# Expert weights loaded as runs of consecutive rows, with a permuted order of contraction

## The chip, the cores and the metric

The kernel runs on one core of one Trainium2 chip. The metric is the device time of one execution in microseconds, the median of several runs. A core has five engines that matter here: PE (TensorE, matmuls; its weight loads are shown apart as PEld), DVE (VectorE), ACT (ScalarE), POOL (GpSimd) and SP (SyncE, which here only issues DMAs). Loads run on 16 DMA engines that all queues share.

## The reference, cut to what matters

Two transformer blocks in float32 over 256 tokens of 1024 channels. The first block is attention, a layer norm, a mixture of experts and a second layer norm. The second block is a gated recurrence with a short convolution, then a feed-forward network. The change touches the mixture of experts:

```python
def moe_ffn(x, w_router, b_router, w_gu, b_gu, w_down, b_down):
    logits = xt @ w_router + b_router              # 256 tokens, 32 experts
    top_logit, top_e = lax.top_k(logits, 4)
    gate = jax.nn.softmax(top_logit, axis=-1)
    ...
    def expert_block(args):                        # xb: an expert's tokens
        h = xb @ w_gu[e] + b_gu[e]                 # w_gu[e]: 1024 x 2048
        h_gate, h_up = jnp.split(h, 2, axis=-1)
        h_gate = jnp.minimum(h_gate, 7.0)
        h_up = jnp.clip(h_up, -7.0, 7.0)
        act = h_gate * jax.nn.sigmoid(1.702 * h_gate) * (h_up + 1.0)
        return act @ w_down[e] + b_down[e]         # w_down[e]: 1024 x 1024
```

Each expert has 8 MiB of gate and up weights and 4 MiB of down weights, all float32, and every expert's weights are read once: 402.65 MB of the 477 MB that the kernel reads from HBM.

## The kernel before

Stages follow one another: attention (to about 115 us of the profile), layer norm and router, the 32 experts (about 140 to 1080 us), the second block (to the end). All large loads are issued by SP from one list, `loads`, in the order in which the weights are used. `pump` (L178) issues the next entries of the list; `weight` (L193) takes a loaded tile and pumps so many entries ahead. A tile is 128 partitions by 16 KiB (2 MiB). During the experts there are ten slots for them, six of pool `wa` (named `w` in the profile) and four of pool `wb`; a load waits until the matmuls on the slot's last content are done.

Expert weights are loaded by `load_rows` (L116). A tile of gate and up weights holds 256 rows of 2048 columns as two blocks: row `k*128 + p` of the piece goes to partition `p`, block `k`, so each partition receives two separate runs of 8 KiB. A tile of down weights holds 512 rows of 1024 columns as four blocks, four runs of 4 KiB to a partition. An expert takes four tiles of the first kind and two of the second. The second block's first weights, `w2`, come by `load_cols` (L105), 512 columns at a time, runs of 2 KiB. Contraction runs over partitions, so a matmul on block `k` needs the activations' channels `k*128 ... k*128+127` on the partitions.

An expert has 64 slots for tokens. Experts go in pairs (a batch). `make_batch` (L681) gathers the tokens of two experts with matmuls by a one-hot matrix: `gather` (L661) takes 128 channels of the normed tokens `h1` as the stationary operand and writes them, channel by partition, to `pgat`; `gathered` (L667) applies the norm's gain and bias on the way to `xs`. `gate_up` (L746) multiplies `xs` by the weights into banks `pg` and `pu` (L764); `swiglu` gives `at`, tokens by partition; `transpose_act` (L770) turns `at` in four pieces of 128 columns with PE (L773), `at` stationary and the identity moving; `down_half` (L780) multiplies by the down weights into `pd` (L786); `combine` (L804) adds the pair's results to the tokens (`pc`, L809). At expert 4 stands a run-time branch, `overflow` (L812), for experts with more than 64 tokens; it is not taken with these inputs, but every engine reads the condition (L815). `turn` (L490) turns `h1` for the router, `turn_router` multiplies the router's weights `wr` by the norm's gain, and `turn_parameters` (L348) turns the gains and biases so that channel `kt*128 + p` stands on partition `p`, column `kt` of `prm`.

A planner orders the instructions of each engine by its own costs and priorities, except in the stretches under `manual_schedule`, where the program's order holds. The experts' loop is left to the planner.

Of the kernel before, what the change touches and what calls it, by code (L numbers as in the profile page):

```python
# [10 lines left out]
F32 = mybir.dt.float32  # L11
# [11 lines left out]
P = 128  # L23
# [27 lines left out]
# columns of the constant table  # L51
# [3 lines left out]
def shape_constants():  # L55
    c = np.zeros((P, C_END), np.float32)
    r = np.arange(P)
    c[:, C_ID:C_ID + P] = np.eye(P)
    c[:, C_TRI:C_TRI + P] = r[:, None] < r[None, :]
    c[:, C_ONE:C_ONE + P] = 1.0  # L60
    c[:, C_IOTA:C_IOTA + P] = r[None, :]
    n = np.arange(256)
    half = BUCKETS // 2
    nf = np.maximum(n, 1).astype(np.float32)
    large = half + (np.log(nf / np.float32(half)) / np.float32(math.log(MAX_DIST / half))
                    * np.float32(BUCKETS - half)).astype(np.int32)
    bucket = np.where(n < half, n, np.minimum(large, BUCKETS - 1))
    onehot = (np.arange(BUCKETS)[:, None] == bucket[None, :]).astype(np.float32)
    # level lv: keys s of the even and queries t of the odd blocks of 2**lv; only those t stand
    masks = np.zeros((P, 7, P // 2), np.float32)  # L70
    s = r[:, None]
    for lv in range(7):
        H = 1 << lv
        t = r[r // H % 2 == 1][None, :]
        masks[:, lv] = (s // (2 * H) == t // (2 * H)) & (s // H % 2 == 0)
    return {"c_main": c, "c_bucket": onehot, "c_masks": masks.reshape(P, 7 * P // 2)}
# [7 lines left out]
def block_kernel(ctx: ExitStack, tc: tile.TileContext, a: dict, out: bass.AP, dbg=None):  # L84
# [14 lines left out]
    # ------------------------------------------------------------------ loads  # L99
# [22 lines left out]
    def load_rows_last(t, w, r0, n):  # L122
        """n = 4 blocks of rows, two of them alone"""
        cols = w.shape[1]
        v = t[:, 0:n * cols].rearrange("p (k c) -> p k c", c=cols)
        for k, m in ((0, 2), (2, 1), (3, 1)):
            nc.sync.dma_start(v[:, k:k + m], w[r0 + k * P:r0 + (k + m) * P, :]
                              .rearrange("(k p) c -> p k c", p=P))
# [14 lines left out]
    def open_room(t):  # L143
        """a slot without a load: room for what is computed"""
        nc.gpsimd.memset(t[:, 0:1], 0.0)
# [9 lines left out]
    for e in range(NE + 1):  # L155
        gu = [(("gu", e, c), load_rows, (w_gu[e], c * 256, 2)) for c in range(4) if e < NE]
        dn = [(("dn", e - 1, c), load_rows, (w_dn[e - 1], c * 512, 4)) for c in range(2) if e > 0]
        loads += dn + gu if e == OVF_AT else gu + dn
    end_moe = len(loads)
    loads[-1] = (loads[-1][0], load_rows_last, loads[-1][2])  # L160
# [43 lines left out]
    # R: 1 + slot of each token within its expert, 0 where it is not routed there  # L204
# [5 lines left out]
    # h1 is written late: its rows hold the tables of the relative bias until then  # L210
# [19 lines left out]
    # the second block's rows take its place  # L230
# [9 lines left out]
    nc.gpsimd.memset(eps_rms, RMS_EPS)  # L240
    R_LNG, R_LNB, R_PMIX, R_PFFN, R_NMIX, R_NFFN = (0, 1), (2, 3), 4, 5, 6, 7

    def bcast_row(psum_ap, r, half):
        """half of row r of `rows` on all partitions"""
        for q in range(2):
            c = 4 * r + 2 * half + q
            mm(psum_ap[:, q * 256:(q + 1) * 256], selb[:, c:c + 1].to_broadcast([96, P]), rows,
               start=True, stop=True)

    def passes(psum_ap, kts, *pairs):  # L250
        """the sum of all products of pairs of operands, pair by pair"""
# [10 lines left out]
    def warm(bank_, n):  # L262
        """n matmuls without a use, that open the clock gate"""
        for _ in range(n):
            mm(bank_[0:1, 0:T], idle, idle.to_broadcast([P, T]), start=True, stop=True)

    # ============================================================ attention
    with ExitStack() as c1:
# [9 lines left out]
        # constants and small parameters for later  # L278
# [8 lines left out]
        # per-channel parameters, 128 channels to a column  # L287
        fw = a["ffn_conv_w_2"][0].rearrange("j (k p) -> (j k) p", p=P)
        for r0, n, src in ((0, 8, a["ln_g"][0, 0:1]), (8, 8, a["ln_b"][0, 0:1])):
            nc.sync.dma_start(raw[r0:r0 + n, 0, :], src.rearrange("o (k p) -> (o k) p", p=P))  # L290
# [6 lines left out]
        # x turned to [channel, token]; matmuls before it and between open the clock gate  # L297
# [25 lines left out]
        nc.sync.dma_start(wr, a["moe_w_router"][0].rearrange("(k p) e -> p k e", p=P))  # L323
# [3 lines left out]
        def split3(dst, src):  # L327
            """dst rows 0.., 32.., 64..: three bf16 parts that sum to src exactly"""
# [19 lines left out]
        def turn_parameters(raw):  # L348
# [3 lines left out]
            V.tensor_copy(prm, pp)  # L352

        def turn_router():
            """the router behind the layer norm's gain and bias: its weights by the gain (wr),
            and its bias with the weights by the norm's bias (br)"""
# [21 lines left out]
        def proj_ch(pool, w, m, xh, xl, psum_ap):  # L378
            """psum [128 columns of w, T] = (columns m of w)^T x^T"""
# [3 lines left out]
        def proj_tok(pool, w, xh, xl, psums):  # L383
            """psums[tt] [128 tokens, 512] = x w for a chunk of 512 columns"""
# [9 lines left out]
        def attend(h, qT, kT):  # L394
# [19 lines left out]
            # columns: keys 0 of queries 0, keys 0 of queries 1, keys 1 of queries 1  # L414
# [48 lines left out]
        def stats(tt):  # L463
            """h1 = ALPHA x + attention and its statistics: mean, variance, 1 / deviation"""
# [14 lines left out]
        def scaled(tt, mv):  # L479
            """h1 = its layer norm but for gain and bias, half by half"""  # L480
# [9 lines left out]
        def turn(tt, hT, g):  # L490
            """half of the channels of a tile, turned to [channel, token]"""
            pt = ps.tile([P, 4, P], F32, name="htp", tag="v", bufs=2)
            for j in range(4):
                kt = 4 * g + j
                nc.tensor.transpose(pt[:, j, :], h1[:, tt, kt * P:(kt + 1) * P], ident)
            nc.scalar.copy(hT[:, 4 * g:4 * g + 4, :], pt)

        def logits(hT, n):
            """... after n matmuls that keep the clock gate open"""
# [8 lines left out]
        def choose(tt, lg):  # L508
            """the experts of a tile's tokens: sel, and one-hot in order"""
# [25 lines left out]
        # the rest for the first tile, then for the second  # L535
# [46 lines left out]
    # ============================================================ experts  # L582
    y = xtok
    with ExitStack() as c2:
# [10 lines left out]
        def gates():  # L595
            """the gates of each token's experts (G), and whether a load exceeds CAP"""
# [19 lines left out]
        def forget_bounds():  # L616
            """lower bound of the forget gates: running sum of the softmax over the layers
            less its first row; and 1 less the bound"""
# [8 lines left out]
        def start_y():  # L627
            """y = ALPHA * the layer norm + the experts' output biases by their gates"""
# [22 lines left out]
        # ---- experts, CAP slots each  # L651
# [9 lines left out]
        def gather(b, pg, kk, tt, j, start, stop):  # L661
            kt = 4 * kk + j
            mm(pg[:, j, :], h1[:, tt, kt * P:(kt + 1) * P],  # L663
# [3 lines left out]
        def gathered(xs, pg, kk):  # L667
            """the gathered channels with the layer norm's gain and bias"""
# [23 lines left out]
        def first_batch(choice):  # L692
            """batch 0, with the slots of the second tile's tokens found on the way"""
# [28 lines left out]
        def weigh_batch(b):  # L722
            """the gates of a batch, [slot, token]"""
# [46 lines left out]
        def transpose_act(at, tag="aT", copy=nc.any.tensor_copy):  # L770
            pt = bank("atp", [P, 4, P], "t")
            for j in range(4):
                nc.tensor.transpose(pt[:, j, :], at[:, j * P:(j + 1) * P], ident)  # L773
# [6 lines left out]
        def down_half(e, aT, pd, c):  # L780
            w = weight(("dn", e, c), AHEAD).rearrange("p (k c) -> p k c", c=D)
            for k in range(4):
                # rows c*512 + k*128 ..: block k of the activations' half c
# [28 lines left out]
        def overflow():  # L812
            """slots CAP.. of every expert, when one of them has more than CAP tokens"""
            n = nc.values_load(cnti[0:1, 0:1], min_val=0, max_val=NE)
            with tc.If(n > 0), tc.For_i(0, n, 1) as e:  # L815
                for g in range(2):
# [9 lines left out]
                    for kk in range(KT // 4):  # L826
                        pg = bank("opgat", [P, 4, P], "m")
                        for j in range(4):
                            kt = 4 * kk + j
                            for tt in range(NT):  # L830
                                mm(pg[:, j, :], h1[:, tt, kt * P:(kt + 1) * P], oh[:, tt],
# [16 lines left out]
                    for kt in range(KT):  # L848
                        for q in range(2):
                            w = p2.tile([P, FF], F32, name="ow", tag="ys")  # L850
                            nc.sync.dma_start(
                                w, w_gu[bass.ds(e, 1), kt * P:(kt + 1) * P, q * FF:(q + 1) * FF]
# [11 lines left out]
                    for kt in range(KT):  # L864
                        w = p2.tile([P, D], F32, name="owd", tag="ys")
                        nc.sync.dma_start(w, w_dn[bass.ds(e, 1), kt * P:(kt + 1) * P, :]
# [16 lines left out]
        def tail_rows():  # L883
            """the second layer norm's rows on all partitions, in place of the first's output"""
# [5 lines left out]
        def open_sums():  # L890
            """banks with y, to which the last pair of experts is added"""
# [7 lines left out]
        def finish_all(prev, at):  # L899
            # the table of the square root, loaded ahead  # L900
# [51 lines left out]
    # ============================================================ second block  # L952
    with ExitStack() as c3:
# [20 lines left out]
        def pre_norm(tt, hh, hl, tag):  # L974
            """a tile's columns of hh + hl [channels, tokens] = rms norm of x1, gains grow"""
# [29 lines left out]
        def post_norm(psums, tt, pg):  # L1005
            """x1 += rms norm of the halves of a tile in psums, gains pg"""
# [28 lines left out]
        # ---------------------------------------------------- token mixing  # L1035
        with ExitStack() as c4:
# [27 lines left out]
            def norm2(tt):  # L1064
                """x1 = layer norm of the sums"""
# [49 lines left out]
            # by head: keys and queries of tile 0, those of tile 1, keys of tile 0 by queries of 1  # L1115
# [59 lines left out]
            # scores [s, t] of each head, by the highest bit in which s and t differ  # L1175
# [60 lines left out]
            # values by scores, scaled by head, turned to [channel, token] and gated  # L1236
# [23 lines left out]
            while rest:  # L1260
                some_units(1)
                if len(rest) < 4:
                    # a block of the convolution's channels is complete
# [25 lines left out]
            # the rest for the first tile, then for the second  # L1289
# [25 lines left out]
        # ---------------------------------------------------- feed-forward  # L1315
        with ExitStack() as c5:
# [4 lines left out]
            def up(j):  # L1321
# [18 lines left out]
                if j == NFB - 1:  # L1340
                    # the table of the square root, loaded ahead
# [91 lines left out]
```

## Time and profile before

| | |
|---|---|
| time, median of 3 runs (lowest, highest) | 1427.29 us (1424.75 to 1427.61) |
| profiled execution: span from first to last instruction | 1422.9 us |
| mean granted TensorE clock | 0.982 |
| PE busy / PEld busy / DVE busy / ACT busy | 1326.0 / 803.4 / 533.2 / 326.4 us |
| read from HBM | 476.70 MB |

The profile gives no time of that execution but its span; 4.4 us lie between the span and the median of the runs. A busy PE is not a PE at its peak: matmuls overlap and their ends are modelled. The chain of waits follows the work that ended last back from the end, piece by piece.

### The profile page before, as it was taken

Reading aid. Unit: us, or ns where it says so; the run is one execution under the profiler, and the core shown is the slowest. Engines: PE = TensorE matmul, PEld = TensorE weight load, DVE = VectorE, ACT = ScalarE, POOL = GpSimd, SP = SyncE. Lnnn points to the kernel's source line nnn. Section 1 sums busy time; section 2 is a strip of 40 time slices with the busy share of each in tenths; the row PEclk is TensorE's granted clock in tenths of the full one; section 3 lists DMA queues with packets and bytes.
Section 4 is the critical chain, followed back from the end, with each engine's and each line's share of the span. In section 5 each row is a group of like instructions: output and inputs, shape, how many; then the busy total and the mean of one; then the engine's idle time right before and its main releaser. Section 6 shows DMA issues by size and latency. Waiting matters only on the chain.

```text
span 1422.9 us, 16930 instructions
## 1 busy us (share of the span) xinstructions
PE 1326.0 (93%) x7160; PEld 803.4 (56%) x7160; DVE 533.2 (37%) x924; ACT 326.4 (23%) x573; POOL 74.3 (5%) x47
## 2 busy tenths in 40 slices
PE   9999998999989999898988989989798999999998
PEld 8887332535343454443533344443234999899997
DVE  4674411122122212222122212112116577777776
ACT  4553000011010000100001000000023445555554
POOL 2510000000000000000000000000002421000000
PEclk9999999999999999999999999999999999999999
DMA  8976999899999999999999999999999314555500
GB/s 260 349 305 263 412 414 419 358 416 415 416 418 416 417 415 416 417 416 417 416 415 416 416 417 417 415 416 416 417 411 380 139 60 164 192 178 184 198 4 30
DMA packets 116180, 478.91 MB, mean 337 GB/s; under 512 B 5284, under 2 KB 32500, under 8 KB 83236
## 3 DMA queue, kind: packets, MB, share of 16 engines
q1 hardware_dynamic: 115988, 477.61, 84.7%
q8 instruction: 58, 0.95, 0.3%
q0 software_dynamic: 112, 0.17, 0.0%
q14 instruction: 22, 0.18, 0.0%
HBM read 476.70 MB, written 1.06 MB: 336 GB/s over the span
## 4 chain that ended last, share of the span: by engine, by line
PE 59%; DMA 17%; DVE 4%; ACT 1%; issue 1%; SPq 0%; DVEq 0%; ACTq 0%
PE pd L786 10%; PE pg L764 10%; PE pu L254 9%; PE pu L764 8%; DMA wb<-in_moe_w_gate_up_dram 6%; DMA w<-in_moe_w_down_dram 5%; PE pq L254 4%; DMA w<-in_moe_w_gate_up_dram 4%; PE pgat L663 4%; PE pc L809 3%; DMA wb<-in_moe_w_down_dram 2%; PE fa L258 1%; PE fa L260 1%; PE fa L259 1%; PE pv L1061 1%; PE px L1201 1%
## 5 line engine op out<-in xcount | busy, mean ns | idle before, releaser
L764 PE MATMUL pg<-w,xs 128*64 128x512 f32 x616 | 181.1, 597 | 6.7 <-DMA w<-in_moe_w_gate_up_dram 6.7
L764 PE MATMUL pu<-w,xs 128*64 128x512 f32 x616 | 180.3, 592 | 0.0
L786 PE MATMUL pd<-w,aT 128*64 128x512 f32 x624 | 154.7, 630 | 3.4 <-DMA w<-in_moe_w_down_dram 2.1
L740 DVE TENSOR_SCALAR sw_g<-pg 128x512 f32<-128x512 f32 x32 | 22.1, 692 | 362.0 <-PE pg L764 362.0
L741 ACT ACTIVATE at<-sw_g 128x512 f32<-128x512 f32 x32 | 20.1, 630 | 529.2 <-DVE sw_g L740 529.2
L764 PE MATMUL pg<-wb,xs 128*64 128x512 f32 x408 | 116.9, 596 | 9.0 <-DMA wb<-in_moe_w_gate_up_dram 9.0
L764 PE MATMUL pu<-wb,xs 128*64 128x512 f32 x408 | 115.8, 592 | 0.0
L795 DVE COPY ys<-pd 64x512 f32<-64x512 f32 x32 | 21.9, 683 | 232.9 <-PE pd L786 232.9
L764 PEld LDWEIGHTS pu<-w,xs 128*64 128x64 f32 x616 | 62.4, 137 | 73.8 <-issue 57.5
L786 PEld LDWEIGHTS pd<-w,aT 128*64 128x64 f32 x624 | 59.1, 144 | 74.9 <-issue 56.6
L764 PEld LDWEIGHTS pg<-w,xs 128*64 128x64 f32 x616 | 58.7, 136 | 74.8 <-issue 56.7
L970 ACT CAST hi<-w 128x1024 fp32r<-128x1024 f32 x75 | 78.4, 1048 | 87.0 <-PE pu L254 40.1
L786 PE MATMUL pd<-wb,aT 128*64 128x512 f32 x400 | 93.8, 605 | 0.1
L971 DVE TENSOR_TENSOR lo<-w,hi 128x1024 fp32r<-128x1024 f32 x60 | 74.0, 1234 | 43.5 <-ACT hi L970 41.1
L971 POOL TENSOR_TENSOR lo<-w,hi 128x1024 fp32r<-128x1024 f32 x15 | 36.4, 2433 | 1030.4 <-DVE st L1068 959.5
L775 ACT COPY aT<-atp 128x512 f32<-128x512 f32 x32 | 18.8, 586 | 271.8 <-PE pd L786 232.6
L663 PEld LDWEIGHTS pgat<-oh,h 128*128 128x128 f32 x512 | 64.2, 205 | 21.5 <-issue 19.1
L663 PE MATMUL pgat<-oh,h 128*128 128x128 f32 x512 | 69.6, 294 | 0.0
L764 PEld LDWEIGHTS pg<-wb,xs 128*64 128x64 f32 x408 | 36.3, 136 | 58.5 <-issue 44.9
L764 PEld LDWEIGHTS pu<-wb,xs 128*64 128x64 f32 x408 | 38.5, 137 | 50.6 <-issue 42.2
L809 PE MATMUL pc<-ys,wT 128*128 128x512 f32 x120 | 57.2, 609 | 2.4 <-DVE ys L795 2.4
L786 PEld LDWEIGHTS pd<-wb,aT 128*64 128x64 f32 x400 | 35.0, 138 | 42.5 <-issue 33.9
(316 smaller groups left out, 1874.9 us busy)
## 6 DMA issues: line engine op xcount, KB each, us to landing
w<-in_moe_w_gate_up_dram SPq DMA_DIRECT2D x77, 2048.0 KB
wb<-in_moe_w_gate_up_dram SPq DMA_DIRECT2D x51, 2048.0 KB
w<-in_moe_w_down_dram SPq DMA_DIRECT2D x38, 2048.0 KB
wb<-in_moe_w_down_dram SPq DMA_DIRECT2D x25, 2048.0 KB
w<-in_ffn_w_up_dram SPq DMA_DIRECT2D x22, 1024.0 KB
w<-in_w_in_dram SPq DMA_DIRECT2D x6, 2048.0 KB
w<-in_a_w_in_dram SPq DMA_DIRECT2D x5, 2048.0 KB
w<-in_ffn_w_down_dram SPq DMA_DIRECT2D x5, 2048.0 KB
```

Source lines behind the costliest of these rows:

```text
L254: mm(psum_ap, lhs[:, kt, :], rhs[:, kt, :], start=(i == 0 and kt == kts[0]), stop=(i == len(pairs) - 1 and kt == kts[-1]))
L258: mm(psum_ap, lh, rh, start=first, stop=False)
L663: mm(pg[:, j, :], h1[:, tt, kt * P:(kt + 1) * P], batches[b][1][:, tt].rearrange("p e s -> p (e s)"), start=start, stop=stop)
L740: V.tensor_scalar(gt, pg, LIMIT, None, op0=OP.min)
L741: act(dst, gt, AF.Sigmoid, scale=SW_ALPHA)
L764: mm(dst[h * CAP:(h + 1) * CAP, :], xs[:, kt, col:col + CAP], w[:, k, c0:c0 + 512], start=False, stop=(kt == KT - 1))
L775: copy(aT, pt)
L786: mm(pd[h][h * CAP:(h + 1) * CAP, :], lhs, w[:, k, h * 512:(h + 1) * 512], start=(c == 0 and k == 0), stop=(c == 1 and k == 3))
L795: (nc.scalar.copy if h else V.tensor_copy)(ys[o:o + CAP, h, :], pd[h][h * CAP:(h + 1) * CAP, :])
L809: mm(pc, lhs[:, tt * P:(tt + 1) * P], ys[:, h, :], start=True, stop=True)
L970: nc.scalar.copy(hi, piece)
L971: (nc.gpsimd if on_pool else V).tensor_sub(lo, piece, f32(hi))
```

## The change

The loads of expert weights put consecutive rows on one partition. `load_run` gives partition `p` of a gate/up tile rows `2p` and `2p+1` of its 256 rows, and partition `p` of a down tile rows `4p` to `4p+3` of its 512: one run of 16 KiB on both sides for each partition. The very last load still comes in three pieces, now of rows `4p`, `4p+1` together, then `4p+2`, then `4p+3`. Block `k` of a tile then holds every second (or fourth) channel, and everything that meets it follows: `gather`, `turn` and the overflow code read `h1` at a step of two elements (`chan`), `transpose_act` reads `at` at a step of four, and the router's weights and the norm's gains and biases are laid out to match, the latter with two more transposes and one more copy. The other lines of the diff take comments away.

```diff
-    def load_rows_last(t, w, r0, n):
+    def load_run(t, w, r0, n):
+        cols = w.shape[1]
+        nc.sync.dma_start(t[:, 0:n * cols], w[r0:r0 + n * P, :]
+                          .rearrange("(p k) c -> p (k c)", k=n))
+    def load_run_last(t, w, r0, n):
         ...
         for k, m in ((0, 2), (2, 1), (3, 1)):
-            nc.sync.dma_start(v[:, k:k + m], w[r0 + k * P:r0 + (k + m) * P, :]
-                              .rearrange("(k p) c -> p k c", p=P))
+            nc.sync.dma_start(v[:, k:k + m], w[r0:r0 + n * P, :]
+                              .rearrange("(p k) c -> p k c", k=n)[:, k:k + m])
...
-        gu = [(("gu", e, c), load_rows, (w_gu[e], c * 256, 2)) ...
-        dn = [(("dn", e - 1, c), load_rows, (w_dn[e - 1], c * 512, 4)) ...
+        gu = [(("gu", e, c), load_run, (w_gu[e], c * 256, 2)) ...
+        dn = [(("dn", e - 1, c), load_run, (w_dn[e - 1], c * 512, 4)) ...
...
+    def chan(kt):
+        c0 = kt // 2 * 2 * P
+        return slice(c0 + kt % 2, c0 + 2 * P, 2)
...
-        for r0, n, src in ((0, 8, a["ln_g"][0, 0:1]), (8, 8, a["ln_b"][0, 0:1])):
-            nc.sync.dma_start(raw[r0:r0 + n, 0, :], src.rearrange("o (k p) -> (o k) p", p=P))
+        lraw = small[0:8, 1536:1792]
+        for r0, src in ((0, a["ln_g"][0, 0:1]), (4, a["ln_b"][0, 0:1])):
+            nc.sync.dma_start(lraw[r0:r0 + 4, :], src.rearrange("o (c f) -> (o c) f", f=256))
...
-        nc.sync.dma_start(wr, a["moe_w_router"][0].rearrange("(k p) e -> p k e", p=P))
+        nc.sync.dma_start(wr.rearrange("p (c k) e -> p c k e", k=2),
+                          a["moe_w_router"][0].rearrange("(c p k) e -> p c k e", p=P, k=2))
...
             V.tensor_copy(prm, pp)
+            pl = ps.tile([P, 2, 2, 4], F32, name="prml", tag="qk", bufs=2)
+            for k in range(2):
+                nc.tensor.transpose(pl[:, k].rearrange("p a c -> p (a c)"), lraw[:, k::2],
+                                    ident[0:8, 0:8])
+            V.tensor_copy(prm[:, 0, 0:16].rearrange("p (a c k) -> p k a c", a=2, k=2), pl)
...
-                nc.tensor.transpose(pt[:, j, :], h1[:, tt, kt * P:(kt + 1) * P], ident)
+                nc.tensor.transpose(pt[:, j, :], h1[:, tt, chan(kt)], ident)
...
-            mm(pg[:, j, :], h1[:, tt, kt * P:(kt + 1) * P],
+            mm(pg[:, j, :], h1[:, tt, chan(kt)],
...
-                nc.tensor.transpose(pt[:, j, :], at[:, j * P:(j + 1) * P], ident)
+                nc.tensor.transpose(pt[:, j, :], at[:, j::4], ident)
```

## Rows read from the trace of the kernel before

**Rows 1.** Page, parts 1 and 2: engines' busy time; slices of 35.6 us.
```profile
PE 1326.0 (93%) x7160; PEld 803.4 (56%) x7160; DVE 533.2 (37%) x924; ACT 326.4 (23%) x573; POOL 74.3 (5%) x47
...
DMA  8976999899999999999999999999999314555500
GB/s 260 349 305 263 412 414 419 358 416 415 416 418 416 417 415 416 417 416 417 416 415 416 416 417 417 415 416 416 417 411 380 139 60 164 192 178 184 198 4 30
```

**Rows 2.** PE's waits, total, times, longest (us), from 560 to 1035 us.
```profile
PE pg L764 <- DMA wb<-in_moe_w_gate_up_dram: 9.0, 8, 1.4
PE pg L764 <- DMA w<-in_moe_w_gate_up_dram: 6.7, 5, 2.1
PE pd L786 <- DMA w<-in_moe_w_down_dram: 2.1, 2, 1.3
```

**Rows 3.** Chain of waits in order of time: start, duration (us), what.
```profile
377.20 3.62 PE pc L809 x8
...
491.91 3.62 PE pc L809 x8
...
565.48 28.43 DMA wb<-in_moe_w_gate_up_dram
...
995.04 34.11 DMA w<-in_moe_w_down_dram
1029.20 3.68 PE pd L786 x16
...
1033.64 3.89 PE pc L809 x8
```

**Rows 4.** Busy time, clock, DMA share and GB/s of chosen stretches (us).
```profile
core 0: us, PE busy (x) PEld busy (x) DVE busy (x) ACT busy (x) POOL busy (x), PEclk, DMA share, GB/s
225.00:245.00 20.00, 18.01 (x74) 5.67 (x70) 5.93 (x9) 1.75 (x3) 0.00 (x0) 1.00 1.01 421
279.00:1029.00 750.00, 684.40 (x3198) 313.67 (x3194) 152.03 (x288) 65.15 (x128) 0.00 (x0) 0.99 1.02 416
...
1049.00:1061.00 12.00, 10.21 (x46) 3.23 (x44) 2.77 (x4) 3.20 (x5) 0.00 (x0) 0.91 1.02 410
1071.00:1100.00 29.00, 22.90 (x110) 13.61 (x107) 19.92 (x27) 9.72 (x20) 9.74 (x4) 0.88 1.04 386
```

**Rows 5.** SP's DMA issues in order of time: start, duration (us), line, load.
```profile
217.60 7.23 SPq L118 DMA_DIRECT2D wb<-in_moe_w_gate_up_dram  x3
227.91 4.54 SPq L118 DMA_DIRECT2D w<-in_moe_w_gate_up_dram  x2
...
1045.12 9.74 SPq L127 DMA_DIRECT2D w<-in_moe_w_down_dram  x3
1054.96 6.15 SPq L113 DMA_DIRECT2D w<-in_w_in_dram  x2
```

**Rows 6.** Page, part 2: packets of all DMAs by size.
```profile
DMA packets 116180, 478.91 MB, mean 337 GB/s; under 512 B 5284, under 2 KB 32500, under 8 KB 83236
```

**Rows 7.** Weight loads of a pair's gathers and a transpose, in order of time.
```profile
603.57 0.42 PEld L773 LDWEIGHTS atp<-cmain,at 128*128 128x128 f32 x4 [0.81 <-issue]
...
616.13 1.41 PEld L663 LDWEIGHTS pgat<-oh,h 128*128 128x128 f32 x12 [0.81 <-issue]
...
621.25 2.31 PEld L663 LDWEIGHTS pgat<-oh,h 128*128 128x128 f32 x20 [0.81 <-issue]
```

**Rows 8.** Chain of waits, first and last level of scores (L1201).
```profile
1134.60 1.85 PE px L1201 x16
...
1161.19 1.73 PE px L1201 x16
```

**Rows 9.** Turning the parameters, in order of time.
```profile
32.55 0.38 PE L351 MATMUL prmp<-cmain,small 128*128 128x128 f32 x2
...
32.97 0.42 DVE L352 COPY prm<-prmp 128x256 f32<-128x256 f32 x1 [7.07 <-PE prmp L351]
```

**Rows 10.** PE's waits, total, times, longest (us), from 245 to 300 us.
```profile
PE pg L755 <- PEq L815: 5.9, 1, 5.9
```

More of the change, by code (lines that the diff above doesn't have):

```diff
@@ L155, in block_kernel @@
     for e in range(NE + 1):
-        gu = [(("gu", e, c), load_rows, (w_gu[e], c * 256, 2)) for c in range(4) if e < NE]
-        dn = [(("dn", e - 1, c), load_rows, (w_dn[e - 1], c * 512, 4)) for c in range(2) if e > 0]
+        gu = [(("gu", e, c), load_run, (w_gu[e], c * 256, 2)) for c in range(4) if e < NE]
+        dn = [(("dn", e - 1, c), load_run, (w_dn[e - 1], c * 512, 4)) for c in range(2) if e > 0]
         loads += dn + gu if e == OVF_AT else gu + dn
     end_moe = len(loads)
-    loads[-1] = (loads[-1][0], load_rows_last, loads[-1][2])
+    loads[-1] = (loads[-1][0], load_run_last, loads[-1][2])
     W2_ORDER = (2, 1, 0, 3, 5, 6, 4)
@@ L830, in overflow @@
                             for tt in range(NT):
-                                mm(pg[:, j, :], h1[:, tt, kt * P:(kt + 1) * P], oh[:, tt],
+                                mm(pg[:, j, :], h1[:, tt, chan(kt)], oh[:, tt],
                                    start=(tt == 0), stop=(tt == NT - 1))
@@ L851, in overflow @@
                             nc.sync.dma_start(
-                                w, w_gu[bass.ds(e, 1), kt * P:(kt + 1) * P, q * FF:(q + 1) * FF]
+                                w, w_gu[bass.ds(e, 1), chan(kt), q * FF:(q + 1) * FF]
                                 .rearrange("o p c -> p (o c)"))
@@ L865, in overflow @@
                         w = p2.tile([P, D], F32, name="owd", tag="ys")
-                        nc.sync.dma_start(w, w_dn[bass.ds(e, 1), kt * P:(kt + 1) * P, :]
+                        nc.sync.dma_start(w, w_dn[bass.ds(e, 1), kt // 4 * 512 + kt % 4:kt // 4 * 512 + 512:4, :]
                                           .rearrange("o p c -> p (o c)"))
```

## The prediction

> **What bounds the kernel now.** I read the page's slices first. From the fifth slice to the thirtieth (142 to about 1067 us) the DMA share is nine tenths or more and the rate stands at 410 to 420 GB/s, but for one dip; PE is at nine tenths too [rows 1]. So the experts' stage has two candidates, and the question is which ends last. PE's waits between 560 and 1035 us name loads of expert weights: 9.0 + 6.7 + 2.1 = 17.8 us [rows 2]. That looks small, and the chain of waits says why it is nevertheless the bound. `pc` (the end of a pair of experts) comes every (491.91 - 377.20) / 2 = 57.36 us at first, with no load in the chain. From 565.48 us on the chain goes through loads, the last of them the down weights that land at 1029.15 us, where `pd` starts at once [rows 3]. From there to the end the chain is PE, DVE and ACT.
>
> Two speeds explain this. A pair reads 2 x 12.58 = 25.17 MB; in the 750 us from 279 to 1029 us the DMA engines are full (share 1.02) at 416 GB/s [rows 4], that is 60.5 us a pair. PE alone needs 57.36 us. At 279 us the slots are full, since just before PE and SP stood at the run-time branch (5.9 us of it is a wait of PE) [rows 10]; PE eats up that lead by 565 us and then runs at the pace of the loads. Over the eleven pairs from 377.20 to 1033.64 us the mean is 59.68 us, so a DMA without any limit would bring no more than 11 x (59.68 - 57.36) = 25.5 us, unless PE itself changes.
>
> **The loads.** The gain hangs on how the rate depends on the run. Of all packets 116,180 - 83,236 = 32,944 are of 8 KiB or more [rows 6]; the gate and up weights alone make 32 x 8 MiB / 8 KiB = 32,768, so a run of 8 KiB goes as one packet, and I take it that one of 16 KiB does too. Three stretches carry one size each, by the loads that SP issued just ahead of them [rows 5]: 225 to 245 us gate and up weights (8 KiB), 421 GB/s; 1049 to 1061 us down weights (4 KiB), 410 GB/s; 1071 to 1100 us `w_in` (2 KiB), 386 GB/s [rows 4]. Per packet and engine (16 x bytes / rate) that is 311.3, 159.8 and 84.9 ns. From 4 to 8 KiB a packet grows by 151.5 ns; two such steps more give 614.3 ns for 16 KiB, 427 GB/s. With the step from 2 to 4 KiB (74.9 ns per 2 KiB) it would be 611.1 ns, 429 GB/s. From the other side, no gain beyond 8 KiB: 421. I take 427, since it continues the nearest step.
>
> An expert is now 1024 packets of 8 KiB and 1024 of 4 KiB, over 16 engines 19.92 + 10.23 = 30.15 us (the 416 GB/s measured make it 30.26); after it is 768 packets of 16 KiB, 768 x 614.3 / 16 = 29.49 us. That is 2.2% less, of 750 us **16.4 us**. With 611.1 ns it is 20.3 us, with 421 GB/s throughout 6.4 us. What is loaded before 279 us doesn't count, as the branch and the full slots set that time; neither does what comes behind 1029 us, where the chain is PE's.
>
> Fewer packets per load also free SP, which is held 2 to 3 us by an issue [rows 5]; nothing waits for it while the engines are full, so nothing. The last load keeps three pieces. The router's weights come in half as many packets and the two small loads of gains in as many bytes: nothing.
>
> **PE's new strides.** No row shows a stationary operand read at a step. Below, the cost is nothing, and no gain is possible, as the same columns are loaded. Above, I let the weight loads double. A pair's 32 gathers load weights in 1.41 + 2.31 = 3.72 us and are paced by them; an expert's four transposes take 0.42 us of such loads [rows 7]. Doubled, a pair costs PE 3.72 us more for the gathers and 0.84 us for the transposes. The nearest row is a moving operand: at the first level of the scores it is read at a step of two elements, at the last contiguously, and 16 matmuls take 1.85 and 1.73 us [rows 8], 8 ns apart each and largely under their weight loads. I take nothing for both, and keep the doubling for the rivals. PE has room: at 427 GB/s with the measured loss a pair takes 60.5 x 0.978 = 59.2 us, 1.8 above its own 57.36; summed from 377 us, PE's floor lies 25.5 - 16.4 = 9.1 us under the loads.
>
> [...]
>
> **The parameters.** Two small transposes and a copy join a chain that now takes 0.38 and 0.42 us [rows 9], at most 0.8 us in a stage that PE fills. DVE's next instructions and the router's bias wait behind the copy; I take 0.3 us.
>
> **Sum.** 16.4 gained, 0.3 lost: 16.1 us. The profiled span of 1422.9 us becomes 1406.8; with the 4.4 us between it and the median, 1427.3 becomes **1411 us**.
>
> **Rivals.**
> 1. *The transposes pay.* If their weight loads double, PE takes over as the bound: 0.84 us on each of 11 pairs (9.2), 0.42 on each of the eight experts before 377 us (3.4) and on the last two (0.8) leave 25.5 - 13.4 = 12 us of gain: 1415 us. [...]
> 2. *No gain beyond 8 KiB* (the runs are cut, or the rate is flat): only the down weights gain, 6.4 us: 1421 us. The rate's steps (+24, +11 GB/s) flatten, which speaks for it; that they follow a fixed cost per packet speaks against it. [...]
> 3. *Nothing.* The planner orders the experts' loop anew by its own costs, and what it puts in a worse place eats a gain of rival 2's size, or the doubled transposes do: within 3 us of 1427.
> 4. *The strided gathers bind PE*, on the other side. `gather` (L663) reads `h1` at a step of two; doubled loads cost 3.72 us a pair, 5 batches before 377 us (18.6) and 11 pairs after (40.9), less the 25.5 us that the loads cover: 34 us slower, 1461 us; with the transposes 47, 1474 us. It decides from an added 25.5 / 16 = 1.6 us per pair on, that is gathers' loads longer by 43%. Their pace, set by weight loads already, speaks for it; rows 8 against it.
>
> **How the numbers follow.** The forecast has 0.46, rival 1 0.15, rival 2 0.16, rival 3 0.08, rival 4 0.15. A change under 0.2% (2.9 us) can't be told from none. Faster: 0.46 + 0.15 + 0.16 = 0.77; same 0.08; slower 0.15. The likeliest case's own range, with 429 GB/s and with 0.8 us for the parameters, is 1407 to 1413. The range goes down to 1404, near PE's floor of 25.5 us, and up over rivals 1 to 3 to 1428; left out are rival 4 and a little below, under 0.2.
>
> **What would show it.** Right: packets of 8 KiB or more fall to about 25,000 while those under 8 KiB fall by 32,768; the rate during the experts goes to 425 to 428 GB/s with the share still at 1.0; `pc` keeps its 57.4 us longer, with loads entering the chain only near 780 us, and waits for loads shrink; weight loads of L663 and L773 keep their pace [rows 7]. Wrong: a rate under 422; gathers' weight loads well over 3.7 us a pair and a pair over 59.7 us; a chain through the experts without loads at a pair time other than 57.4.

## The result, and the profile after

The changed kernel takes **1407.2 us** (median of 4 runs, 1403.0 to 1417.6) where the kernel before took 1427.5 us beside it (4 runs, 1424.8 to 1429.2): a ratio of 0.986, with a 95% interval of 0.982 to 0.990. Six later runs gave 1406.0 against 1428.5 (0.985, 0.981 to 0.989). Forecast were 1411 us, a ratio of 0.989.

The page of the changed kernel: the rate in its slices, and the packets.

```profile
GB/s 258 344 307 281 397 425 428 367 428 427 427 426 427 427 426 428 426 426 427 428 426 426 426 429 428 425 426 427 427 413 331 121 69 173 181 192 195 184 1 31
DMA packets 74948, 478.91 MB, mean 341 GB/s; under 512 B 4764, under 2 KB 31972, under 8 KB 50196
```

The same bytes go in 74,948 packets where it was 116,180 [rows 6]; 24,752 of them are of 8 KiB or more, and those under 8 KiB fell by 33,040. Behind the dip of the run-time branch the rate in the experts is 425 to 429 GB/s, where the slices of before stood at 415 to 418 [rows 1].

PE's waits between 560 and 1035 us (in all, times, longest): the largest, which was as large before, and the only one for a load, 1.2 us. Before, three rows of waits for loads made 17.8 us [rows 2]:

```profile
PE pu L775 <- DVE at L763: 26.5, 14, 2.0
...
PE pd L806 <- DMA w<-in_moe_w_down_dram: 1.2, 2, 0.7
```

Two stretches of the changed kernel (columns as in rows 4): one that carries only gate and up weights, now 16 KiB packets, and the whole experts' stage:

```profile
225.00:245.00 20.00, 18.47 (x78) 6.10 (x74) 5.32 (x9) 2.38 (x4) 0.00 (x0) 1.00 1.01 428
...
279.00:1008.00 729.00, 680.22 (x3202) 327.11 (x3198) 151.97 (x288) 65.07 (x128) 0.00 (x0) 1.00 1.01 427
```

Its chain of waits in order of time, to the end of the experts:

```profile
378.67 3.63 PE pc L829 x8
438.10 3.62 PE pc L829 x8
495.82 3.62 PE pc L829 x8
...
901.58 3.62 PE pc L829 x8
959.31 3.62 PE pc L829 x8
...
971.75 36.47 DMA w<-in_moe_w_down_dram
1008.27 3.68 PE pd L806 x16
1012.71 3.89 PE pc L829 x8
```

Two things are to be seen. The last `pc` comes at 1012.71 us where it was 1033.64 [rows 3]: 20.9 us earlier, and from there to the end the two executions are alike (spans 1402.4 and 1422.9 us, 20.5 apart). And the chain runs on PE alone to 971.75 us, 57.73 us a pair (59.4 in two of them, see the last section); one load is left in it, for which PE waits 0.7 us at most. Before, loads were in it from 565.48 us on.

The stage begins behind the run-time branch, where SP issues nothing for 23 to 24 us. SP's last issue ahead of it and its first behind it (start, how long the issue held SP, what), of the kernel before:

```profile
239.90 2.59 SPq L118 DMA_DIRECT2D w<-in_moe_w_down_dram  x1
266.74 0.39 SPq L118 DMA_DIRECT2D w<-in_moe_w_gate_up_dram  x1
```

and of the changed kernel:

```profile
240.75 0.33 SPq L125 DMA_DIRECT2D w<-in_moe_w_down_dram  x1
264.05 0.35 SPq L125 DMA_DIRECT2D w<-in_moe_w_gate_up_dram  x1
```

This splits the 20.9 us. From SP's first load behind the branch to the landing of the down weights that end the loads' part of the chain it was 1029.15 - 266.74 = 762.4 us; now it is 971.75 + 36.47 - 264.05 = 744.2 us. That is **18.2 us from the loads' rate** behind the branch.

The other 2.7 us are a stage that begins earlier, and that is the loads' rate too, ahead of the branch. SP goes on only when every load that it has issued has landed (its waits at the branch's line, L815, are 23.0 us in all): in the trace the last one lands at 266.07 us before and at 263.38 us after, and 0.7 us later SP issues the next. In between the DMA engines stand empty (the last two columns are their busy share and GB/s), before and after:

```profile
266.00:267.00 1.00, 1.00 (x8) 0.63 (x5) 0.00 (x0) 0.00 (x0) 0.00 (x0) 1.00 0.00 0
```

```profile
263.40:264.40 1.00, 1.00 (x8) 0.64 (x5) 0.00 (x0) 0.00 (x0) 0.00 (x0) 1.00 0.00 0
```

That load landed 26.2 us behind its issue before and 22.6 us now, as what was queued ahead of it comes faster. The rate from 150 to 240 us, before and after:

```profile
150.00:240.00 90.00, 88.33 (x409) 31.41 (x407) 25.53 (x44) 8.12 (x15) 0.00 (x0) 1.00 1.01 414
```

```profile
150.00:240.00 90.00, 88.47 (x409) 32.18 (x408) 25.64 (x43) 8.11 (x15) 0.00 (x0) 1.00 1.00 424
```

Of these 3.5 us, 0.85 are lost to a later issue of that load. That the issue held SP 2.59 us before and 0.33 us now plays no part, since SP waits for the landing in any case.

### The profile page after: what moved, and what is told of

The parts are those of the page before. It is cut to its first block, busy times and chain, and to the rows that moved or that the text cites. A ratio compares the mean times of both kernels' runs of the same rounds, so it can differ in the third digit from the quotient of the medians.

```text
span 1402.4 us, 16939 instructions
## 1 busy us (share of the span) xinstructions
PE 1321.1 (94%) x7162; PEld 816.7 (58%) x7162; DVE 533.1 (38%) x925; ACT 326.0 (23%) x573; POOL 75.3 (5%) x47
## 2 busy tenths in 40 slices
DMA packets 74948, 478.91 MB, mean 341 GB/s; under 512 B 4764, under 2 KB 31972, under 8 KB 50196
## 4 chain that ended last, share of the span: by engine, by line
PE 72%; DVE 5%; DMA 3%; ACT 1%; issue 1%; DVEq 0%; ACTq 0%
PE pd L806 14%; PE pg L784 13%; PE pu L784 12%; PE pu L266 9%; PE pq L266 4%; PE pgat L683 4%; PE pc L829 3%; DMA w<-in_moe_w_down_dram 3%; PE fa L270 1%; PE fa L272 1%; PE fa L271 1%; PE atp L793 1%; DVE at L763 1%; DVE sw_g L762 1%; PE pu L775 1%; PE pv L1081 1%
## 5 line engine op out<-in xcount | busy, mean ns | idle before, releaser
L806 PE MATMUL pd<-w,aT 128*64 128x512 f32 x624 | 147.9, 606 | 2.6 <-DMA w<-in_moe_w_down_dram 1.2
L815 DVE COPY ys<-pd 64x512 f32<-64x512 f32 x32 | 21.9, 683 | 227.3 <-PE pd L806 227.3
L795 ACT COPY aT<-atp 128x512 f32<-128x512 f32 x32 | 18.7, 585 | 266.7 <-PE pd L806 226.9
L784 PEld LDWEIGHTS pg<-wb,xs 128*64 128x64 f32 x408 | 39.8, 137 | 44.1 <-issue 30.9
```

The lines of the kernel that those rows point to most:

```text
L784: mm(dst[h * CAP:(h + 1) * CAP, :], xs[:, kt, col:col + CAP], w[:, k, c0:c0 + 512], start=False, stop=(kt == KT - 1))
L795: copy(aT, pt)
L806: mm(pd[h][h * CAP:(h + 1) * CAP, :], lhs, w[:, k, h * 512:(h + 1) * 512], start=(c == 0 and k == 0), stop=(c == 1 and k == 3))
L815: (nc.scalar.copy if h else V.tensor_copy)(ys[o:o + CAP, h, :], pd[h][h * CAP:(h + 1) * CAP, :])
```

## The experiments

The measure "from SP's first load behind the branch to the landing of the down weights that end the loads' part of the chain" is used throughout; it is the same load in every kernel up to experiment 4. It is steadier than the time of a run, since the attention stage ahead of it differs by some 10 us between executions: SP's first load behind the branch came at 266.74 us in the kernel before and at 279.26 us in the kernel of experiment 9, which is the same up to there.

**Experiments 1 to 3: the packets alone.** Partitions keep the same consecutive rows and PE its strides, but a load writes its rows in reverse order into the tile, so that a run ends with every row. The first reverses both kinds of weights (8 and 4 KiB packets, as before), the second gate and up weights only, the third down weights only; PE reads block `1 - k` or `3 - k` to match:

```diff
-        nc.sync.dma_start(t[:, 0:n * cols], w[r0:r0 + n * P, :]
-                          .rearrange("(p k) c -> p (k c)", k=n))
+        nc.sync.dma_start(t[:, 0:n * cols].rearrange("p (k c) -> p k c", c=cols),
+                          w[r0:r0 + n * P, :].rearrange("(p k) c -> p k c", k=n)[:, ::-1])
```

> Same rows on each partition and the same strided reads by PE as in the changed kernel, but the blocks of a tile are stored in reverse order, so a run is one row again: packets of 8 KiB (gate and up) and 4 KiB (down). Theory (the gain is the size of the packet): the rate during the experts falls back from 426 to about 416 GB/s, the down weights that PE last waits for land near 1026 to 1029 us instead of 1008, and the time is 1424 to 1428 us. Rival (the gain is that a partition reads neighbouring rows of HBM): rate and time stay, 426 GB/s and 1405 to 1410 us.

> Only the gate and up tiles have their blocks reversed (8 KiB packets); down tiles keep runs of 16 KiB. Theory: an expert's packets take 19.92 + 256 x 614.3 / 16 = 29.75 us instead of 30.15 before and 29.49 in the changed kernel, so about 10 us of the 750 are kept and with the earlier start behind the branch some 12: 1413 to 1418 us, about 422 GB/s. Rival (neighbouring rows): as the changed kernel, 1405 to 1410 us.

> Only the down tiles have their blocks reversed (4 KiB packets); gate and up tiles keep runs of 16 KiB. Theory: 512 x 614.3 / 16 + 10.23 = 29.89 us an expert, 6.5 us of the 750 kept, some 8 with the earlier start behind the branch: 1418 to 1422 us, about 420 GB/s. The gains of this kernel and of the one with only the gate and up tiles reversed should add up to the whole. Rival (neighbouring rows): 1405 to 1410 us.

Measured: 1427.2, 1418.3 and 1420.0 us (10 runs each), ratios to the kernel before 0.999 (0.996 to 1.002), 0.992 (0.988 to 0.995) and 0.994 (0.991 to 0.997); the second lies 0.3 us above what was expected of it. Their pages count 115,652, 91,332 and 99,269 packets. For each stand, in three fences, the stretch 300 to 1000 us (last column GB/s), the last load in its chain of waits, and SP's first load behind the branch. Both reversed:

```profile
300.00:1000.00 700.00, 645.30 (x3006) 306.42 (x3006) 143.34 (x273) 60.50 (x119) 0.00 (x0) 0.99 1.02 416
```

```profile
1005.37 34.34 DMA w<-in_moe_w_down_dram
```

```profile
277.11 0.39 SPq L126 DMA_DIRECT2D w<-in_moe_w_gate_up_dram  x1
```

Gate and up weights reversed:

```profile
300.00:1000.00 700.00, 650.81 (x3054) 313.52 (x3054) 147.19 (x281) 62.74 (x124) 0.00 (x0) 0.99 1.01 422
```

```profile
994.14 33.93 DMA w<-in_moe_w_down_dram
```

```profile
275.98 0.40 SPq L126 DMA_DIRECT2D w<-in_moe_w_gate_up_dram  x1
```

Down weights reversed:

```profile
300.00:1000.00 700.00, 649.53 (x3050) 312.47 (x3052) 146.76 (x280) 63.17 (x125) 0.00 (x0) 0.99 1.01 421
```

```profile
992.94 39.21 DMA w<-in_moe_w_down_dram
```

```profile
277.48 0.36 SPq L129 DMA_DIRECT2D w<-in_moe_w_gate_up_dram  x1
```

| kernel | GB/s | first load to landing | less than before |
|---|---|---|---|
| before | 416 | 762.4 us | |
| both reversed | 416 | 1039.71 - 277.11 = 762.6 us | -0.2 us |
| gate and up reversed | 422 | 1028.07 - 275.98 = 752.1 us | 10.3 us |
| down reversed | 421 | 1032.15 - 277.48 = 754.7 us | 7.7 us |
| changed kernel | 427 | 744.2 us | 18.2 us |

With the packets cut back to their old sizes the whole gain is gone, although every partition still reads neighbouring rows. Long down packets alone bring 10.3 us, long gate and up packets alone 7.7 us, and 10.3 + 7.7 = 18.0 us is close to the 18.2 that both bring together. So the size of the packet is the cause, and the two parts add up.

**Experiment 4: PE without the strides.** The changed kernel, with contiguous reads of `h1` and of the activations, so that channels meet other rows of the weights:

```diff
-            mm(pg[:, j, :], h1[:, tt, chan(kt)],
+            mm(pg[:, j, :], h1[:, tt, kt * P:(kt + 1) * P],
...
-                nc.tensor.transpose(pt[:, j, :], at[:, j::4], ident)
+                nc.tensor.transpose(pt[:, j, :], at[:, j * P:(j + 1) * P], ident)
```

> The changed kernel, but the gathers and the four transposes of an expert read h1 and the activations contiguously as before; channels then meet the wrong weight rows, so the output is not the reference's. Weight loads of the gathers go back to 3.72 us a pair, those of a transpose to 0.42 us an expert, and a pair without waits from 57.7 to 57.36 us. Theory (the loads still set the end of the stage): 0 to 2 us faster than the changed kernel, and waits for loads grow instead. Rival (PE has become the bound): 16 x 0.36 = 6 us faster, near 1401 us.

Measured: 1414.9 us (4 runs, 1409.1 to 1417.7), ratio 0.990 (0.984 to 0.995), overlapping that of the changed kernel. The last load in its chain, and SP's first load behind the branch:

```profile
977.24 37.91 DMA w<-in_moe_w_down_dram
```

```profile
270.64 0.35 SPq L125 DMA_DIRECT2D w<-in_moe_w_gate_up_dram  x1
```

1015.15 - 270.64 = 744.5 us, the 744.2 of the changed kernel: with the loads as they are, at the same 427 GB/s, PE's shorter weight loads gain nothing. The time was expected 0 to 2 us below the changed kernel and came 7.7 us above it; in the two profiles, whose spans are 4.9 us apart, SP's first load comes 6.6 us later, so that difference lies ahead of the experts. Over the ten pairs ahead of the last one PE took as long as in the changed kernel (580.3 and 580.6 us): four of them took 59.0 us there and the others 57.4, where two of the changed kernel's took 59.4 (last section) and the others 57.73.

**Experiments 5 to 8: the branch.** During the branch the loads run dry for some microseconds (61 GB/s from 264 to 268 us of the kernel before). Three kernels put it ahead of expert 24 (`OVF_AT = 24` for 4): the kernel before, the changed one, and the changed one with contiguous reads. The eighth is the changed kernel once more.

> The kernel before, with the run-time branch ahead of expert 24 in place of expert 4. Theory (the experts' stage ends when its bytes have come at the rate of their packets; at expert 4 SP stands at the branch while the queue holds only some 20 us of loads, and the rate falls to 61 GB/s for 4 us): at expert 24 PE has lost its lead, so the slots are less full when SP stops, SP comes to the branch late, and what it has issued may or may not cover the stop. If it covers it, the hole of 4 to 5 us goes and the time is 1422 to 1424 us. Rival (the hole is cover for nothing: the branch costs the loads the same wherever it stands): 1426 to 1429 us. Rival on the other side (with PE right behind the loads, the stop of some 22 us on PE and the loads' hole add up): 1430 to 1440 us.

> The changed kernel with the run-time branch ahead of expert 24 in place of expert 4. Theory: the loads lead PE's end by little now (a pair of experts takes 58.95 us of loads and 57.7 us of PE), so that a hole of 4 to 5 us taken out of the loads gives at most what PE leaves, 0 to 5 us: 1402 to 1408 us. If the branch's cost is the same wherever it stands: 1405 to 1410 us. If PE's stop and the loads' hole add up: 1412 to 1425 us.

> The changed kernel with the branch ahead of expert 24, and with PE reading h1 and the activations contiguously (channels then meet other rows of the weights, so the values computed are not the reference's; the instructions and bytes are the same in number). It tells whether PE's strided weight loads cost anything once the loads are eased. Theory (strides cost 0.36 us a pair of experts, hidden while the loads are the bound): within 2 us of the kernel with the strided reads and the late branch where the loads still end last, up to 6 us below it where PE does. Rival (strides cost nothing anywhere): within 1 us of it in every case.

> The changed kernel itself, for the spread between executions and for the place of the restart behind the branch. Theory (18.2 us of its gain are the rate of the packets, and 2.7 us of the profiled gain are how soon SP comes back behind the branch, which varies between executions): 1404 to 1412 us, and from SP's first load behind the branch to the landing of the down weights that end the loads' part of the chain 743 to 746 us, wherever in the span that branch falls. Rival (the earlier restart belongs to the change): SP's first load behind the branch falls 2 to 3 us earlier than in the kernel before, again.

Measured: 1428.0 us (12 runs; ratio to the kernel before 1.000, 0.998 to 1.003), then 1404.3 (0.982, 0.978 to 0.986), 1411.0 (0.986, 0.983 to 0.990) and 1406.0 us (0.985, 0.981 to 0.989), 6 runs each. My theory that a late branch spares the loads fell. The stretch around the late branch, of the kernel before with it:

```profile
850.00:880.00 30.00, 29.80 (x155) 15.16 (x153) 8.00 (x17) 3.35 (x7) 0.00 (x0) 1.00 0.83 332
```

and around the early one, of the kernel before:

```profile
250.00:280.00 30.00, 29.38 (x142) 18.88 (x144) 6.67 (x19) 2.72 (x6) 0.00 (x0) 0.89 0.88 347
```

Against 416 GB/s, 332 for 30 us are 6.1 us of loads lost, and 347 are 5.0: the branch costs about the same at both places. The late branch in the changed kernel makes no difference that its runs can tell. The seventh was expected within 2 us of the sixth or below it and came 6.7 us above, with intervals that overlap; no run tells whether that is more than the spread. The changed kernel's second profile, SP around the branch:

```profile
240.46 0.33 SPq L125 DMA_DIRECT2D w<-in_moe_w_down_dram  x1
263.44 0.35 SPq L125 DMA_DIRECT2D w<-in_moe_w_gate_up_dram  x1
```

The earlier restart came back (263.44 us, 3.3 us ahead of before), so here the rival holds. The moment alone says little, as it moves with the attention stage (263.4 to 270.6 us in the five profiles with this layout, long packets of both kinds and the early branch). The time from SP's last issue ahead of the branch to its first load behind it says more: 26.2 to 26.8 us in the three profiles that have both old packet sizes (before, experiments 1 and 9), 24.0 us with long down packets alone (experiment 2), 25.3 us with long gate and up packets alone (experiment 3), and 23.0 to 24.3 us in those five. So it belongs to the packets. In this execution no load is in the chain behind 250 us; but the load that ended the loads' part of the chain in the first one, the 150th behind the branch, lands at 1007.54 us here, 744.1 us behind SP's first load, inside the expected 743 to 746.

**Experiments 9 to 11: who ends last now.** If PE and the loads end together, easing the loads must bring the kernel before down to PE's floor and the changed kernel hardly at all. In three kernels every other expert from 5 to 29 uses the first half of its down weights twice, so 13 loads go:

```diff
-        dn = [(("dn", e - 1, c), load_run, (w_dn[e - 1], c * 512, 4)) for c in range(2) if e > 0]
+        dn = [(("dn", e - 1, c), load_run, (w_dn[e - 1], c * 512, 4)) for c in range(2) if e > 0 and not (c and e - 1 in SAME)]
...
-            w = weight(("dn", e, c), AHEAD).rearrange("p (k c) -> p k c", c=D)
+            w = kept.pop(e, None)
+            if w is None:
+                w = weight(("dn", e, c), AHEAD).rearrange("p (k c) -> p k c", c=D)
+            if e in SAME and c == 0:
+                kept[e] = w
```

> The kernel before with 13 of its 64 loads of down weights left out (every other expert from 5 to 29 uses the first half of its down weights for both halves, so the values are not the reference's; the matmuls are the same in number). A pair of experts then reads 23.1 MB, 55.5 us at 416 GB/s, less than PE's 57.4 us. Theory (before, the loads ended last, and 25.5 us was all that PE left under them): 1400 to 1404 us. Rival (packets of 4 and 8 KiB cost PE something by themselves, beside the rate): over 1410 us.

> The changed kernel with the same 13 loads left out (values not the reference's). Theory (after the change PE and the loads end within 1 to 2 us of each other): 1402 to 1407 us, no more than 3 us below the changed kernel, and 3 to 6 us above the kernel before with the same loads left out, as PE's strided reads cost 0.36 us a pair of experts. Rival (the loads are still well behind PE): over 8 us below the changed kernel. Rival (the strides cost PE nothing): equal to the kernel before with the same loads left out, within 1 us.

> The changed kernel with the same loads left out and with contiguous reads of h1 and of the activations (the channels meet other rows of the weights; values not the reference's). Theory: within 2 us of the kernel before with the same loads left out, and 3 to 6 us below the changed kernel with them left out; PE's pairs of experts 0.36 us shorter. Rival (the strides cost PE nothing): pairs equal within 0.05 us.

Measured (6 runs each): **1399.1**, **1403.8** and **1399.2 us**, with ratios to the kernel before of 0.977 (0.972 to 0.982), 0.983 (0.979 to 0.988) and 0.980 (0.976 to 0.984). The first is 0.9 us below its range, the others are as expected. Rows of `pc` from each chain, in which no load stands behind the branch any more. Before, with fewer loads:

```profile
385.23 3.82 PE pc L815 x8
...
1013.82 1.12 PE pc L815 x2
```

Changed, with fewer loads:

```profile
551.33 3.82 PE pc L835 x8
609.04 3.82 PE pc L835 x8
```

Changed, with fewer loads and contiguous reads:

```profile
486.56 3.82 PE pc L835 x8
543.88 3.82 PE pc L835 x8
```

A pair is 57.32 us of PE with contiguous reads and 57.71 with the strides, 0.39 us more. It is the gathers and the transposes, whose weight loads (PEld) take longer and their matmuls (PE) with them. From 280 to 1000 us, by line and form (busy us, mean ns of one), in the changed kernel:

```profile
L683 PEld LDWEIGHTS pgat<-oh,h 128*128 128x128 f32 x416 | 50.8, 196 | 19.5 <-issue 18.7 <-DVE sw_g L760 0.8
...
L793 PEld LDWEIGHTS atp<-cmain,at 128*128 128x128 f32 x100 | 13.9, 209 | 20.3 <-issue 20.3
```

```profile
L683 PE MATMUL pgat<-oh,h 128*128 128x128 f32 x416 | 55.4, 287 | 0.0
...
L793 PE MATMUL atp<-cmain,at 128*128 128x128 f32 x100 | 18.7, 309 | 0.0
```

and with fewer loads and contiguous reads:

```profile
L684 PEld LDWEIGHTS pgat<-oh,h 128*128 128x128 f32 x416 | 48.2, 191 | 19.5 <-issue 18.7 <-DVE sw_g L761 0.8
...
L794 PEld LDWEIGHTS atp<-cmain,at 128*128 128x128 f32 x100 | 10.5, 140 | 20.3 <-issue 19.5 <-DVE wT L756 0.8
```

```profile
L684 PE MATMUL pgat<-oh,h 128*128 128x128 f32 x416 | 52.8, 281 | 0.0
...
L794 PE MATMUL atp<-cmain,at 128*128 128x128 f32 x100 | 16.4, 286 | 0.0
```

A pair has 32 gathers and eight transposes. PE is busy (55.4 - 52.8) / 13 = 0.20 us longer with a pair's gathers and (18.7 - 16.4) / 12.5 = 0.18 us longer with its transposes, 0.38 of the 0.39 us. The changed kernel's own pairs, 57.73 us, are those of its twin with fewer loads: since the change PE sets the pace, and the loads end with it to within 2 us. A version that beats it needs a faster PE and faster loads at once. The runs bound what either brings alone: contiguous reads nothing (experiment 4), fewer loads 1406.0 - 1403.8 = 2.2 us, which is inside the spread of the runs. Experiment 11 has both and takes 1399.2 us, with values that are not the reference's.

## Why the prediction was right

**The bound.** Right. The whole gain comes from the stage whose loads ended last. Without a limit by the loads I allowed 25.5 us over the eleven pairs; the kernel before with fewer loads takes 1013.82 - 385.23 = 628.6 us for them, where it was 656.4 [rows 3], 27.8 us less.

**The rate.** The price of a packet was right: 427 GB/s were forecast for 16 KiB, and 427 to 428 came, where rival 2 had 421. The term was a little small, 16.4 us for 18.2. The same ratio of the two sums of packets, 29.49 / 30.15, over the 762.4 us from SP's first load instead of 750 gives 16.7; the last 1.5 us are 0.2% of the rate, less than one GB/s (by the sums 417 and 427 GB/s, measured 416 and 427). Experiments 1 to 3 show that it is the packets, 10.3 us by the down weights and 7.7 us by the gate and up weights. The fixed cost per packet that I set against rival 2 is an estimate from rows 4: 159.8 ns for 4 KiB, less the 151.5 ns that 4 KiB more take, leaves 8.3 ns.

**The loads ahead of 279 us.** I left them out, "as the branch and the full slots set that time". This step of the sum was wrong. The branch sets that time by waiting for the loads: SP goes on when the last one has landed. In the two profiles the loads ran on from an issue of SP at 140.4 and 140.7 us to that landing, 125.7 us before and 122.7 us after, the same 2.4% as behind the branch. These 3.0 us, begun 0.3 us later, are the 2.7 us between 18.2 and 20.9.

**SP.** I put SP's shorter issues at nothing, and that was right, but the "2 to 3 us by an issue" was a misreading. The first two rows of rows 5 have several issues and hold the waits for a free slot between them too; the row of a single one behind the branch has 0.39 us before and 0.35 us after. The 2.59 us ahead of the branch were a longer hold, and nothing waited for it.

**PE's strides.** I took them as nothing; they cost 0.39 us a pair, 4.3 us over eleven pairs. That is under half of what rival 1 gave the transposes alone (0.84), and far from the 1.6 us a pair from which rival 4 decides, since the gathers' loads grew by 2.6% and not by 43%. That it moved no time is luck, as the room just sufficed: PE's floor with the strides lies 25.5 - 4.3 = 21.2 us under the kernel before (23.5 by the 27.8 above), and the loads gained 20.9. Of the signs that I named for a wrong forecast, one came: a chain without loads, at 57.73 us a pair instead of 57.4. The forecast's time holds since the two limits meet there, and not because PE's cost was read rightly. In the experts the step of four takes a transpose's weight load from 140 to 209 ns, half as much again where I let it double, and the step of two a gather's from 191 to 196 ns; the transposes in the last section pay 145 to 211 ns for a step of two.

**When loads enter the chain.** Forecast near 780 us, found at 971.75 us and in the second profile not at all. PE's lead behind the branch is eaten by the difference of the two paces. Before that was 60.5 - 57.36 = 3.1 us a pair, and it lasted the five pairs from 279 to 565 us, so the lead was some 15.7 us. I set 59.2 against 57.36; it is 25.17 MB / 427 GB/s = 58.9 against 57.73, 1.2 us a pair, and 15.7 / 1.2 = 13 pairs outlast the stage.

**The rest.** Rival 3 (the planner's order, or strides that eat the gain) falls with experiment 1: with the old packet sizes and everything else changed the time is 0.999 of before. The 0.3 us of the parameters lie below what the runs can tell, and no run isolates them. The forecast of 1411 us, 0.989 of before, lies inside both intervals of the changed kernel.

## What to carry to other kernels

Where the DMA engines are full, price a change of layout by its packets: read the time of a packet at two or three sizes off stretches that carry one size each, continue the line, and sum (here 16.4 us, for 18.2 measured). Then price everything else that the layout touches in the second engine, however small, because a gain in the first bound ends where the second begins: here a stride that cost 0.39 us a pair used up what had been left over. And look for the places where the queue runs dry, such as a run-time branch, and at what ends the wait there: here it is the landing of the last load, 0.7 us ahead of SP's next issue, so that what is loaded ahead of the branch counts too.

## What the runs showed of the hardware

**A step of two can cost a weight load as much as a step of four.** The transposes of `turn` ahead of the experts read `h1` at a step of two since the change (100 to 240 us, by line and form). Before:

```profile
L495 PEld LDWEIGHTS htp<-cmain,h 128*128 128x128 f32 x16 | 1.9, 145 | 0.1
```

After:

```profile
L515 PEld LDWEIGHTS htp<-cmain,h 128*128 128x128 f32 x16 | 2.2, 211 | 0.1
```

145 to 211 ns is what the experts' transposes pay for a step of four. The gathers, which read the same tile at the same step, pay 5 ns; contiguously they took 191 ns already. What tells the two apart was not tried.

**Where a pair takes 1.7 us longer, it is PE's clock.** In the changed kernel most pairs take 57.73 us, and two take 59.4 us, as the one that ends at 438.10 us in its chain. Two stretches within that pair (the third column from the right is the granted clock), and PE's row between them (in brackets the idle time ahead, and what ended it):

```profile
401.00:405.00 4.00, 2.01 (x7) 1.24 (x9) 2.85 (x7) 1.69 (x5) 0.00 (x0) 0.81 0.98 418
405.00:409.00 4.00, 4.00 (x16) 2.00 (x12) 0.00 (x0) 0.00 (x0) 0.00 (x0) 0.77 1.03 430
```

```profile
402.99 0.40 PE L775 MATMUL pu<-bgu,selb 96*64 96x512 bf16 x1 [2.01 <-DVE at L763]
```

PE stood 2.01 us for DVE, and the clock then lost (0.19 + 0.23) x 4 us = 1.7 us, that is 3.4 us at 0.50, the lower of the two levels that it shows in this stage (it reads 0.50 from 403.5 to 406.5 us). It is what that pair takes longer. The wait alone does not decide it: the same wait of 2.01 us comes in each of ten pairs, and behind eight of them the clock stayed at the upper level, 1.00, as in the next pair:

```profile
462.42 0.40 PE L775 MATMUL pu<-bgu,selb 96*64 96x512 bf16 x1 [2.01 <-DVE at L763]
```

```profile
462.00:466.00 4.00, 3.58 (x17) 1.98 (x17) 1.28 (x3) 0.14 (x1) 0.00 (x0) 1.00 1.01 430
```

What tells the two apart, no run shows. Now that PE sets the pace, these waits for DVE (26.5 us between 560 and 1035 us, and as much before) are the next place to look.
